# Moving the output-weight sums into the input projection, loading the out projection's first halves one step earlier than their split, and two tiles for kk and v, in a hybrid encoder layer

## The chip, the cores and the metric

The kernel runs on one core of a Trainium2 chip. The metric is the device time of one execution in microseconds, lower being better. The core has five engines that work through queues of their own: TensorE (PE; its weight loads are listed as PEld), VectorE (DVE), ScalarE (ACT), GpSimd (POOL) and SyncE (SP). In this kernel SP issues nearly all the transfers between main memory and the on-chip buffers.

## The reference

One layer over 2048 tokens of width 1024, in fp32. The part that the change touches is the token mixing:

```python
u = rms_norm(h, g_mix_pre[l])
z = u @ w_in[l]
qa, ka, va, qh, fh, ih, gh = jnp.split(z, IN_SPLITS, axis=-1)
ya = swa_with_sinks(qa, ka, va, sinks[l])        # windowed attention, chunks of 64
yh = hgrn2(qh, fh, ih, gh, lb_all[l], hgrn_onorm[l])
y = jnp.concatenate([ya, yh], axis=-1) @ w_out[l]
h = h + rms_norm(y, g_mix_post[l])
...
# cross-attention to 256 memory tokens, then a SwiGLU feed-forward part
```

`hgrn2` is a gated linear recurrence in chunks of 64 tokens with 4 heads of 128:

```python
f = lbf + (1.0 - lbf) * jax.nn.sigmoid(f_logit)
kf = 1.0 - f
b = jnp.cumsum(jnp.log(f) in chunks)
A = einsum(qc * exp(b - b_mid), kc * exp(b_mid - b)), causal
kv = einsum(kc * exp(b_last - b), vc)
S_t = exp(b_last) * S_{t-1} + kv
o = A @ vc + (qc * exp(b)) @ S_prev
output = rms_norm(o, onorm_g) * silu(g)
```

## The kernel before

**Products.** Every fp32 operand is split into a high and a low part, and each product takes three matmuls (L1131, L1132 and L1133 in the big products, L156, L157 and L158 elsewhere). A split is made of a copy to the high part (L987 on ACT, L989 on POOL) and a subtraction for the low part (L990 on DVE). The big products are block products with seven sub-products instead of eight: their operands are sums and differences of blocks of the matrices. The four derived weight combinations of a product (keys 5, 7, 6 and 4) are worked out once by `combined`, which loads blocks, adds or subtracts them on DVE (L1034) and stores the result to main memory with `store` (L78). For the out projection's weights `w_out` they go to the tensor `out_s`: 8 operations of 128 x 1024 elements, because each combination is made in two halves. The big products' schedule is the generator `phases`: it runs over jobs, over their blocks, and over the seven (or fewer) sub-product steps of a block. A job can carry generators that run *beside* its blocks, one step of them after each product step; `put` in `combined` is held behind the newest ACT and DVE instruction at that point.

**Stages.** From 0 to about 250 us `in_first` projects the first 1024 tokens: thirteen pairs of output columns, the first four blocks without combined weights (kinds q, u and v), then nine blocks of seven products. From block 4 on some blocks close with a chain: DVE adds the parts of the output (L644), ACT takes a tanh (L650 or L656), POOL scales (L652), and `decays` takes a logarithm on ACT (L730), which needs another table loaded, and goes on from there. ACT's L1146 copies a partial product out of the accumulator so that PE may go on to the next (PE's L1131 waits for it). Weight tiles come in as `sraw`.

From 250 to about 615 us three generators run in turn, one step of each per pair of token chunks: the windowed attention `swa` (L804 to L853; its last part writes `ys` by L852 on ACT and L853 on DVE, and stores it to `y_d`), the recurrence `hgrn`, and the projection of one column for the second 1024 tokens, `in_proj` (the `cols`). The columns' outputs are the io tiles `z`, of which there are two; they are stored to `z_d`. In the second half of that stage, from pair 8 of the attention on, the generator of the `out_s` sums was run beside these, four steps after each attention pair, with the io tiles `u` and `x` as its two buffers.

From about 615 to 775 us the recurrence's pairs 8 to 15 run beside `fold_cross`, which prepares the cross-attention's weights from the memory (transposes L124 of `raw` weights or memory rows into accumulator banks; L126 on ACT and L127 on DVE copy and split these; L156 to L158 multiply). At each of those pairs one step of the out projection's prologue is taken: from pair 2 on it loaded half of a block of `w_out` into an io tile `z` and split it at once into the out projection's first operands (`T<-z`, L987 on ACT and L990 on DVE). After 775 us come the out projection, the cross-attention and the feed-forward part, all by `phases`.

**A pair of the recurrence.** `hgrn_front` loads k1 (the F columns, for the scores), qq, kk (the F columns again, for the state) and v, each by SP from `z_d`. The scores are L886 on PE, with copies L887 on DVE and L888 on ACT into `atz`. POOL multiplies kk by a decay (L894), PE transposes kk (L897) and v (L902) into banks, and ACT copies them out (kt L899, vt L903 and L904). `hgrn_state` then takes the product L913 of kt and vt, POOL scales the old state (L914), DVE adds (L915); `hgrn_out` is L925 and L926 on PE and L930 to L935 on ACT, POOL and DVE. k1, kk and v had one tile each, qq two.

**Order.** A scheduler with a simulated timeline puts the instructions in an order when the kernel is built; each engine then works through its own list in that order, and SP's list of transfers is in order too. A transfer is issued by SP only when the tile that it fills has been released, and a transfer that waits holds up those behind it in SP's list.

Of the kernel before, what the change touches and what calls it, by code (L numbers as in the profile page):

```python
# [11 lines left out]
F32 = mybir.dt.float32  # L12
# [6 lines left out]
P = 128  # L19
T = 2048  # L20
D = 1024
# [12 lines left out]
C_KA, C_VA, C_QH, C_FH, C_IH, C_GH = 512, 640, 768, 1280, 1792, 2304  # L34
# [14 lines left out]
class Layer:  # L49
# [144 lines left out]
    def mix(self):  # L194
        tc, I = self.tc, self.I
        kw = dict(reuse_waits="tile")
        with contextlib.ExitStack() as left:
            def pool(name, at, **k):
                return at.enter_context(tc.tile_pool(name=name, bufs=1, **k, **kw))

            self.mc = pool("mc", left)
            self.r_x = self.cst.tile([P, NT], F32, name="r_x")
            with (
                tc.tile_pool(name="t1", bufs=3, **kw) as self.ts,
                tc.tile_pool(name="t2", bufs=3, **kw) as self.tb,
                tc.tile_pool(name="s1", bufs=2, side="right", **kw) as self.st_pool,
                contextlib.ExitStack() as at,
            ):
                self.banks(at, "ps1", **MOST)
                self.raws = 3  # L210
                u = self.in_first()
            self.banks(left, "ps2", **FOUR)
            self.hg = pool("hg", left)
            self.wp = pool("wp", left)
            self.io = pool("io", left)
            with tc.tile_pool(name="sw", bufs=1, side="right", **kw) as self.sw:
                self.zero_tiles()
                swa = self.swa(range(NT), lambda n: "st" if n < NPB else "sth")
                hgrn = self.hgrn(range(NPB), "h")
                cols = self.in_proj(1, u)  # L220
                next(cols)
                for _ in range(NPB + 1):
                    next(swa)
                    next(hgrn)
                    next(cols)
                for _ in hgrn:
                    pass
                self.out_sums, side = self.sums("out_s", self.w_out, 4, lambda: self.io_tile("u"), lambda: self.io_tile("x"))
                side = side()
                next(side)  # L230
                pairs = self.hgrn(range(NPB, NT), "gt")
                for i, _ in enumerate(swa, NPB + 2):
                    next(cols)
                    if i == NT + 1 - 0:
                        next(pairs)
                    for _ in range(4):
                        next(side, None)
                for _ in cols:
                    pass
            phases = self.phases(self.jobs(), None, lambda: self.io_tile("z"))  # L240
            with tc.tile_pool(name="xp", bufs=1, side="right", **kw) as self.xp:
                fold = self.fold_cross()
                for _ in range(2):
                    next(fold)
                for i, _ in enumerate(pairs, 1):
                    for _ in range(2):
                        next(fold)
                    if 2 <= i < 10:
                        next(phases)
                for _ in fold:  # L250
                    pass
            left.close()
            with (
                tc.tile_pool(name="t3", bufs=3, **kw) as self.ts,
                tc.tile_pool(name="t4", bufs=3, **kw) as self.tb,
                tc.tile_pool(name="s3", bufs=2, side="right", **kw) as self.st_pool,
                contextlib.ExitStack() as at,
            ):
                self.banks(at, "ps3", **MOST)
                self.raws = 4  # L260
                for _ in phases:
                    pass
# [188 lines left out]
    def in_first(self):  # L451
# [65 lines left out]
        def fetch():  # L517
            for s in range(2):
                for q in range(2):
# [11 lines left out]
                  for i, p in enumerate(self.ORDER)]  # L531
# [1 line left out]
        plain = [b[1:4] + ([],) for b in blocks[:2]]  # L533
        blocks[:2] = ([(k, stream, out, lambda: iter(()), keep) for k, (stream, out, _, keep) in zip("qu", plain)]
                      + [("v", lambda kind: iter([None]), out, after, keep) for _, out, after, keep in plain])
        phases = self.phases([(lambda i, j, a, n: raw[i, j][:, a:a + n, :], 4, blocks, None, {})], T)
        PE, ACT, DVE, POOL = (getattr(mybir.EngineType, e) for e in ("PE", "Activation", "DVE", "Pool"))
        next(phases)
        self.turns("h", 36)
# [45 lines left out]
        u = []  # L585
# [270 lines left out]
    def hgrn_front(self, n, kinds):  # L856
        nc, ph = self.nc, self.hg
        t0 = n * P
        z = self.z_d
        kinds = itertools.cycle(kinds)  # L860

        def get(t, c):
            self.load(t, z[c:c + 512, t0:t0 + P].rearrange("(h p) t -> p h t", p=P))
            return t

        def new(tag, bufs=1, w=P):
            return ph.tile([P, 4, w], F32, tag=tag, name=f"{tag}{n}", bufs=bufs)

        def c8(ap):
            return ap.rearrange("p h (c t) -> p (h c) t", t=64)  # L870

        k1 = get(new("k1"), C_FH)
        qq = new("qq", 2, 192)
        q1 = get(qq[:, :, 0:P], C_QH)
        kk = get(new("kk"), C_FH)
        v = get(new("v"), C_IH)
        g1 = self.G1[:, n, :].unsqueeze(2).broadcast_to([P, 4, 64])

        nc.gpsimd.tensor_tensor(qq[:, :, P:192], qq[:, :, 64:P], g1, ALU.mult)

        at = self.atz[n % 2]
        for i in range(2):
            ps = self.bank(next(kinds))[:, 0:384].rearrange("p (h t) -> p h t", h=2)
            hs = slice(2 * i, 2 * i + 2)
            for r in range(2):
                nc.tensor.matmul(ps[:, r, :], k1[:, 2 * i + r, :], qq[:, 2 * i + r, :], start=True, stop=True)  # L886
            nc.vector.copy_predicated(at[:, hs, :], self.cmask.unsqueeze(1).broadcast_to([P, 2, P]), ps[:, :, 0:P])  # L887
            nc.scalar.activation(at[0:64, hs, 64:P], ps[0:64, :, P:192], AF.Copy)  # L888

        q6 = new("q6", 2)  # L890
        nc.gpsimd.tensor_tensor(q6.rearrange("p h (c t) -> p h c t", t=64), q1.rearrange("p h (c t) -> p h c t", t=64),
                                self.G[:, n, :, :].unsqueeze(3).broadcast_to([P, 4, 2, 64]), ALU.mult)

        nc.gpsimd.tensor_tensor(kk[:, :, 0:64], kk[:, :, 0:64], g1, ALU.mult)  # L894
        ps = self.bank(next(kinds))
        for h in range(4):
            nc.tensor.transpose(ps[:, h * P:(h + 1) * P], kk[:, h, :], self.ident)  # L897
        kt = new("kt")
        nc.scalar.activation(kt, ps.rearrange("p (h t) -> p h t", h=4), AF.Copy)  # L899
        ps = self.bank(next(kinds))  # L900
        for h in range(4):
            nc.tensor.transpose(ps[:, h * P:(h + 1) * P], v[:, h, :], self.ident)  # L902
        vt = new("vt", 2)  # L903
        nc.scalar.activation(vt, ps.rearrange("p (h t) -> p h t", h=4), AF.Copy)  # L904
        return q6, at, kt, vt
# [313 lines left out]
    def phases(self, jobs, first, prologue=None):  # L1219
# [42 lines left out]
        def split(g):  # L1262

            if pending and pending[0][0] <= g:
                _, k, f = pending.pop(0)
                f()
                left[k] -= 1
                return True
            return False

        def half(g, tile):

            if current[0] is None:
                if not queue:
                    return False
                free = min(slots, key=lambda s: s[1])
                if free[1] > g:
                    return False
                n, p, _ = k = queue.pop(0)
                slots.remove(free)  # L1280
                slots.append((free[0], uses[k][-1], free[2]))
                self._n += 1
                dst = (self.big if free[0] == "A" else self.tb).tile(
                    [P, 2, 4, 512], F32R, tag="big" if free[0] == "A" else "T", name=f"T_{self._n}",
                    bufs=4 if free[0] == "A" else 3)[:, :, :jobs[n][1]]
                T[k] = dst
                left[k] = 2
                current[:] = [(k, self.resident(fetch(n, tile), jobs[n][1], p, dst, keep[n], jobs[n][3] is not None)), 0]
            k, f = current[0]
            pending.append((g + lag(k), k, next(f)))  # L1290
            current[1] += 1
            if current[1] == 2:
                next(f, None)
                current[0] = None
            return True
# [28 lines left out]
                made[0] += 1  # L1324

        if not first:
            for i in range(8):
                half(-1, prologue)
                split(len(steps))
                yield  # L1330
        stream(0)
        yield
# [458 lines left out]
```

## Time and profile before

| | us |
|---|---|
| median of 3 runs | 2554.95 |
| lowest and highest | 2553.55 and 2556.43 |
| profiled execution | 2550.01 |
| its span | 2548.3 |
| its mean granted PE clock | 0.997 |

All rows of the profile come from the one profiled execution, which is 4.94 us under the median of the three runs. Names like `psm L1131` give the tile that an instruction writes and its line in the code; `T<-z` reads "T is made from z". Times are microseconds from the start of the span, unless a row gives ns.

### The profile page before, as it was taken

Reading aid. Unit: us, or ns where it says so; the run is one execution under the profiler, and the core shown is the slowest. Engines: PE = TensorE matmul, PEld = TensorE weight load, DVE = VectorE, ACT = ScalarE, POOL = GpSimd, SP = SyncE. Lnnn points to the kernel's source line nnn. Section 1 sums busy time; section 2 is a strip of 40 time slices with the busy share of each in tenths; the row PEclk is TensorE's granted clock in tenths of the full one; section 3 lists DMA queues with packets and bytes.
Section 4 is the critical chain, followed back from the end, with each engine's and each line's share of the span. In section 5 each row is a group of like instructions: output and inputs, shape, how many; then the busy total and the mean of one; then the engine's idle time right before and its main releaser. Section 6 shows DMA issues by size and latency. Waiting matters only on the chain.

```text
span 2548.3 us, 34324 instructions
## 1 busy us (share of the span) xinstructions
PE 2504.8 (98%) x12006; PEld 2092.8 (82%) x12006; DVE 1792.1 (70%) x2871; ACT 1261.6 (50%) x2635; POOL 364.6 (14%) x540
## 2 busy tenths in 40 slices
PE   9999999999999999999999999999999999999998
PEld 8878888877997778878878888888888888878886
DVE  8885488987556989988876555576566557574766
ACT  5553466655555566566753333353333335443543
POOL 4231234321311112102200000000000000000022
PEclk9999999999999999999999999999999999999999
DMA  6455655865887996867954522254465434564786
GB/s 201 146 165 178 192 154 170 230 204 146 259 292 275 316 335 189 274 206 226 333 200 146 177 91 87 74 203 148 160 210 195 144 117 159 180 188 106 228 177 151
DMA packets 387885, 486.33 MB, mean 191 GB/s; under 512 B 22272, under 2 KB 283392, under 8 KB 387712
## 3 DMA queue, kind: packets, MB, share of 16 engines
q1 hardware_dynamic: 381664, 462.12, 55.9%
q0 software_dynamic: 6048, 22.02, 5.0%
q8 instruction: 94, 1.54, 0.2%
q14 instruction: 79, 0.65, 0.1%
HBM read 317.34 MB, written 166.72 MB: 190 GB/s over the span
## 4 chain that ended last, share of the span: by engine, by line
PE 51%; DVE 2%; DMA 1%; issue 1%; ACT 1%; POOL 0%; SPq 0%; DVEq 0%; POOLq 0%; ACTq 0%
PE psm L1133 17%; PE psm L1131 17%; PE psm L1132 17%; DVE T L990 0%; DVE S L990 0%; ACT junk L1504 0%; PE pss L1390 0%; DMA out_dram<-row 0%; DMA row<-d_s 0%; DMA row<-in_w_down_dram 0%; DMA u_d<-row 0%; DMA sraw<-in_w_gate_dram 0%; DVE sum L1106 0%; ACT S L987 0%; ACT T L987 0%
## 5 line engine op out<-in xcount | busy, mean ns | idle before, releaser
L1131 PE MATMUL psm<-T,S 128*128 128x512 f32 x2680 | 1034.1, 390 | 13.3 <-ACT part L1146 7.2
L1132 PE MATMUL psm<-T,S 128*128 128x512 f32 x2680 | 1042.3, 390 | 4.0 <-DVE T L990 3.9
L1133 PE MATMUL psm<-T,S 128*128 128x512 f32 x2680 | 1029.4, 389 | 4.1 <-DVE S L990 4.1
L1131 PEld LDWEIGHTS psm<-T,S 128*128 128x128 f32 x2680 | 503.0, 188 | 125.9 <-ACT part L1146 11.9
L1132 PEld LDWEIGHTS psm<-T,S 128*128 128x128 f32 x2680 | 503.2, 188 | 110.5 <-DVE T L990 7.3
L1133 PEld LDWEIGHTS psm<-T,S 128*128 128x128 f32 x2680 | 503.1, 188 | 110.6 <-DVE S L990 6.3
L987 ACT ACTIVATE S<-sum 128x512 fp32r<-128x512 f32 (+1 forms) x370 | 224.0, 620 | 371.5 <-PE psm L1133 267.3
L990 DVE TENSOR_TENSOR S<-sraw,S 128x512 fp32r<-128x512 f32 (+1 forms) x315 | 211.5, 679 | 218.8 <-ACT S L987 215.8
L1146 ACT ACTIVATE part<-psm 128x512 f32<-128x512 f32 x285 | 168.6, 596 | 251.9 <-PE psm L1133 230.9
L990 DVE TENSOR_TENSOR S<-sum,S 128x512 fp32r<-128x512 f32 (+1 forms) x388 | 257.4, 673 | 42.1 <-ACT S L987 38.3
L987 ACT ACTIVATE S<-sraw 128x512 fp32r<-128x512 f32 (+1 forms) x300 | 184.7, 618 | 110.8 <-PE psm L1133 106.0
L1537 POOL DMA_DIRECT2D y_d<-row x16 | 14.1, 879 | 1077.9 <-DVE row L1721 1027.6
L990 DVE TENSOR_TENSOR T<-row,T 128x1024 fp32r<-128x1024 f32 (+1 forms) x112 | 131.0, 1183 | 30.2 <-ACT T L987 29.2
L157 PE MATMUL psg<-u,whi 128*128 128x512 f32 x320 | 128.3, 401 | 0.0
L158 PE MATMUL psg<-u,wlo 128*128 128x512 f32 x320 | 127.6, 399 | 0.0
L156 PE MATMUL psg<-u,whi 128*128 128x512 f32 x320 | 127.5, 399 | 0.0
L1504 ACT ACTIVATE junk<-row 128x512 f32<-128x512 f32 x160 | 99.6, 624 | 40.6 <-DVE row L1526 20.6
L987 ACT ACTIVATE T<-row 128x1024 fp32r<-128x1024 f32 (+1 forms) x112 | 113.3, 1031 | 7.5 <-DMA row<-d_s 4.3
L1672 DVE TENSOR_TENSOR row<-psm,part 128x512 f32<-128x512 f32 x66 | 43.7, 687 | 66.9 <-PE psm L1133 66.9
L1681 DVE TENSOR_TENSOR part<-psm,part 128x512 f32<-128x512 f32 x66 | 43.8, 687 | 60.1 <-PE psm L1133 59.8
L1721 DVE TENSOR_TENSOR row<-psm,part 128x512 f32<-128x512 f32 x72 | 49.1, 688 | 49.5 <-PE psm L1133 49.4
L814 ACT ACTIVATE S<-S,w_mn 128x256 f32<-128x256 f32 (+1 forms) x128 | 63.0, 496 | 29.6 <-DVE w_mn L810 29.2
(363 smaller groups left out, 3562.2 us busy)
## 6 DMA issues: line engine op xcount, KB each, us to landing
sraw<-in_w_gate_dram SPq DMA_DIRECT2D x44, 512.0 KB, 3.6
sraw<-in_w_up_dram SPq DMA_DIRECT2D x44, 512.0 KB, 3.7
hid_d<-row SPq DMA_DIRECT2D x44, 512.0 KB, 2.7
sraw<-hid_d SPq DMA_DIRECT2D x32, 512.0 KB, 4.2
sraw<-in_w_in_dram SPq DMA_DIRECT2D x44, 256.0 KB, 4.0
z_d<-pair SPq DMA_DIRECT2D x20, 512.0 KB, 3.4
raw<-in_w_in_dram SPq DMA_DIRECT2D x20, 512.0 KB, 4.8
z_d<-z SPq DMA_DIRECT2D x20, 512.0 KB, 4.0
```

The costliest lines, as they stand in the source:

```text
L156: nc.tensor.matmul(ps, ah, bh, start=(i == 0), stop=False)
L157: nc.tensor.matmul(ps, ah, bl, start=False, stop=False)
L158: nc.tensor.matmul(ps, al, bh, start=False, stop=(i == n - 1))
L814: nc.scalar.activation(s[:, r, o:], s[:, r, o:], AF.Exp, bias=mn[:, i:i + 1], scale=-1.0, accum_out=den[:, i:i + 1])
L987: self.nc.scalar.activation(hi, raw, AF.Copy)
L990: self.nc.vector.tensor_tensor(lo, raw, f32(hi), ALU.subtract)
L1131: nc.tensor.matmul(ps, s[:, 0, k, :], t[:, 0, k, :], start=st, stop=False, **kw)
L1132: nc.tensor.matmul(ps, s[:, 0, k, :], t[:, 1, k, :], start=False, stop=False, **kw)
L1133: nc.tensor.matmul(ps, s[:, 1, k, :], t[:, 0, k, :], start=False, stop=sp, **kw)
L1146: nc.scalar.activation(t, ps, AF.Copy)
L1504: self.nc.scalar.activation(junk, a, AF.Square, scale=float(D) ** -0.5, accum_out=to)
L1721: nc.vector.tensor_tensor(d, a, b, ALU.add)
```

## The change

Three edits, with no change to what is computed:

1. The generator of the `out_s` sums leaves the loop of attention and columns. It is now made in `in_first` and given to `phases` as work beside block 4, so that its steps run after the product steps of blocks 4 to 8. Its two buffers are tiles of their own, `wa` and `wb`, one each.
2. The out projection's prologue has nine steps instead of eight: step i loads half i and splits half i − 1. It is driven from the first of the pairs 8 to 15 on (`i < 10`) where it was driven from the second (`2 <= i < 10`), so each split stands in the pair where it stood.
3. kk and v of the recurrence have two tiles each.

```diff
-                self.out_sums, side = self.sums("out_s", self.w_out, 4, lambda: self.io_tile("u"), lambda: self.io_tile("x"))
-                side = side()
-                next(side)
                 pairs = self.hgrn(range(NPB, NT), "gt")
                 for i, _ in enumerate(swa, NPB + 2):
                     next(cols)
                     if i == NT + 1 - 0:
                         next(pairs)
-                    for _ in range(4):
-                        next(side, None)
...
-                    if 2 <= i < 10:
+                    if i < 10:
                         next(phases)
...
+        def weight_tile(tag):
+            self._n += 1
+            return self.st_pool.tile([P, D], F32, tag=tag, name=f"{tag}_{self._n}", bufs=1)
+
+        self.out_sums, side = self.sums("out_s", self.w_out, 4, lambda: weight_tile("wa"), lambda: weight_tile("wb"))
-        phases = self.phases([(lambda i, j, a, n: raw[i, j][:, a:a + n, :], 4, blocks, None, {})], T)
+        phases = self.phases([(lambda i, j, a, n: raw[i, j][:, a:a + n, :], 4, blocks, None, {4: [side]})], T)
...
-        kk = get(new("kk"), C_FH)
-        v = get(new("v"), C_IH)
+        kk = get(new("kk", 2), C_FH)
+        v = get(new("v", 2), C_IH)
...
-            for i in range(8):
-                half(-1, prologue)
-                split(len(steps))
+            for i in range(9):
+                if i < 8:
+                    half(-1, prologue)
+                if i:
+                    split(len(steps))
                 yield
```

## The prediction

> **What bounds the kernel now.** I read the page's busy times first, then the windows by stage, then PE's waits, and then the rows around the work that moves.
>
> ```profile
> span 2548.3 us, 34324 instructions
> ...
> PE 2504.8 (98%) x12006; PEld 2092.8 (82%) x12006; DVE 1792.1 (70%) x2871; ACT 1261.6 (50%) x2635; POOL 364.6 (14%) x540
> ```
>
> TensorE (PE) is busy for 2504.8 of 2548.3 us. The change removes no matmul, so it can win only PE's idle time, 2548.3 − 2504.8 = 43.5 us over the whole span, and time in which PE runs at a lower clock. The recurrence with everything beside it lies between 440 and 775 us:
>
> ```profile
> 440.00:530.00 90.00, 88.73 (x483) 74.77 (x482) 78.62 (x166) 53.52 (x142) 31.67 (x43) 1.00 0.86 251
> 530.00:615.00 85.00, 83.26 (x442) 69.59 (x441) 71.61 (x193) 52.60 (x149) 14.32 (x32) 1.00 0.44 134
> 615.00:660.00 45.00, 41.61 (x296) 38.59 (x295) 28.10 (x38) 24.59 (x52) 6.45 (x8) 0.96 0.90 244
> 660.00:710.00 50.00, 48.13 (x398) 47.15 (x398) 22.63 (x39) 24.88 (x75) 21.85 (x28) 1.00 0.75 241
> 710.00:775.00 65.00, 64.47 (x449) 58.92 (x449) 33.41 (x42) 39.28 (x76) 3.45 (x5) 1.00 0.83 288
> ```
>
> The columns are the stretch, its length, then busy time of PE, weight load, VectorE (DVE), ScalarE (ACT) and GpSimd (POOL), PE's granted clock, the DMA share and GB/s. PE's idle time is 1.27 + 1.74 + 3.39 + 1.87 + 0.53 = 8.8 us: no more than that can be won there, beside the clock of 0.96 in the third row. Which waits make it up, PE's waits tell (first for 615 to 775 us, the last two for 440 to 615 us):
>
> ```profile
> PE pst L902 <- DMA v<-z_d: 2.6, 1, 2.6
> PE pst L902 <- ACT whi L126: 1.1, 1, 1.1
> PE psg L897 <- DVE W L915: 0.8, 2, 0.5
> PE pst L925 <- ACT atz L888: 0.7, 1, 0.7
> ...
> PE psh L849 <- DVE ptl L844: 1.3, 2, 1.0
> PE psh L805 <- DVE ys L853: 0.7, 1, 0.7
> ```
>
> Each line names what waited, what released it, the total, the number of times and the longest.
>
> **Second tiles for kk and v.** With one tile, pair 9's v can only be loaded when pair 8's four transposes at L902 are done. The place in the timeline (PE, then ACT), the windows around it, how long the loads of the tile z take from issue to landing, and a window of the input projection, of which I need the matmuls' pace:
>
> ```profile
> 627.59 0.60 PE L124 MATMUL psh<-ident,u 128*128 128x128 f32 x4
> 630.78 1.04 PE L902 MATMUL pst<-ident,v 128*128 128x128 f32 x4 [2.59 <-DMA v<-z_d]
> ...
> 630.18 1.06 ACT L987 ACTIVATE T<-z 128x1024 fp32r<-128x1024 f32 x1 [3.50 <-DMA z<-in_w_out_dram]
> 631.15 0.58 ACT L126 ACTIVATE mT<-pss 128x512 fp32r<-128x512 f32 x1
> ...
> 628.00:631.00 3.00, 0.41 (x4) 0.25 (x3) 0.53 (x2) 0.81 (x1) 0.00 (x0) 0.98 1.12 231
> 631.00:635.00 4.00, 3.86 (x18) 2.98 (x17) 3.72 (x7) 4.00 (x9) 0.00 (x0) 0.59 0.95 297
> 635.00:640.00 5.00, 5.00 (x46) 5.00 (x45) 2.72 (x4) 1.65 (x10) 3.37 (x5) 1.00 0.95 288
> ...
> DMA to landing us min/median/max: 3.6/5.0/8.3
> ...
> 150.00:200.00 50.00, 49.05 (x216) 40.28 (x215) 38.55 (x55) 21.77 (x36) 14.28 (x19) 1.00 0.60 189
> ```
>
> In the built order of the changed kernel v of pairs 8 and 9 are issued one behind the other on SP, ahead of the last stores of the window attention, so the 2.6 us go. Behind the stall the clock is 0.59 for 4 us, which loses 0.41 × 4 = 1.6 us; at 1.00 again afterwards. Without the stall that loss should go too, but ACT is busy for 4.00 of those 4 us, so PE may meet ACT instead: between 0 and 1.6 us, and I take 1.2, nearer to the clock's row, because the rows after it show PE back at 46 instructions in 5 us. The Trainium skill, "TensorE: Matmul & The Clock Gate", section "What's actually happening", says that the clock halves after an idle window of some 3.4 us; the stall here is shorter, 2.6 us, and the clock fell all the same. By the page's rule alone this term would be 0, and the sum 1.2 us smaller; I go by the row.
>
> What is late next is ACT. In the rows above ACT waits 3.50 us for a loaded weight tile z, and the four copies of L126 stand behind that split. In the new order the second split T<-z stands behind these four copies. The first stands ahead of some 44 projection matmuls, which at 49.05/216 = 227 ns (last row) are 10 us, more than a z load takes (3.6 to 8.3 us), so its wait is covered. But the new order also puts the first L156 of the memory projection ahead of L897: it needs all four L126 copies, 4 × 0.58 = 2.3 us of ACT behind the transposes, while PE has 12 small products and transposes left to run behind the last of these, 1.3 us at 5.00/46 = 109 ns. I charge 0.8 us for that (0 to 2.3).
>
> kk: its multiplication on POOL no longer waits for a load that itself waits for the pair before:
>
> ```profile
> POOL kk L894 <- DMA kk<-z_d: 20.9, 5, 16.6
> ...
> ACT T L987 <- DMA z<-in_w_out_dram: 17.5, 8, 3.7
> ```
>
> The POOL queue holds the state products of L914 behind kk, and DVE's L915 behind those, so the 0.8 us of PE at L897 should go (0 to 0.8). The other 20 us of POOL's waiting hide behind PE already and are worth nothing.
>
> **First halves split a pair late.** The 8 loads, 8 splits on ACT and 8 on DVE stay, in the same pairs; only a load is now issued one step ahead of its split. ACT's 17.5 us of waiting (second row above) mostly go. They cost PE only where a PE wait stands behind them in ACT's queue: the 0.7 us at atz L888, and perhaps the 1.1 us at L126. I take 0.7 (0 to 1.8). SP gets the same 12 transfers, the first still behind the last stores of the projection, because there are two z tiles and the projection's outputs use them.
>
> **The sums, leaving.** Eight additions on DVE, 6 MB of loads and 4 MB of stores leave 440 to 530 us. One of them delays a PE wait visibly:
>
> ```profile
> L1034 DVE TENSOR_TENSOR u<-u,x x6: 1198/1214/1224, 448.1 to 521.9; 128x1024 f32<-128x1024 f32 x6
> ...
> 521.91 1.22 DVE L1034 TENSOR_TENSOR u<-u,x 128x1024 f32<-128x1024 f32 x1 [2.76 <-DMA out_s<-u]
> 523.05 0.68 DVE L853 TENSOR_TENSOR ys<-psh,ys 64x512 f32<-64x512 f32 x1
> ...
> DMA to landing us min/median/max: 2.6/4.2/6.6
> ```
>
> An addition starts at 521.91, and ys of L853, for which PE waited 0.7 us, follows at its end. With the additions gone I count that 0.7, and 0.3 of the 1.27 us idle in 440:530 for the seven others: 1.0 us (0 to 1.3).
>
> **The sums, arriving.** Eight additions of 1.214 us, 9.7 us of DVE, now fall beside blocks 4 to 8 of the input projection, between about 90 and 160 us of the old time. There DVE is the fullest engine after PE:
>
> ```profile
> 90.00:100.00 10.00, 10.00 (x45) 8.27 (x45) 4.52 (x8) 3.76 (x7) 2.65 (x4) 1.00 0.74 225
> ...
> 160.00:170.00 10.00, 9.05 (x40) 7.21 (x39) 10.00 (x13) 8.42 (x13) 5.64 (x5) 1.00 0.62 207
> sum 70.00, PE 66.40 PEld 53.73 DVE 65.31 ACT 45.51 POOL 31.89; mean PE 9.49 PEld 7.68 DVE 9.33 ACT 6.50 POOL 4.56
> ...
> PE psm L1131 <- ACT part L1146: 3.6, 4, 1.2
> ```
>
> The sum row is for 100 to 170 us: DVE 65.31 of 70. By the built order two additions fall before or at 100 us, where DVE has 5.5 us free in ten, and six behind: 65.3 + 6 × 1.214 = 72.6 us in 70. So DVE falls 2.6 us behind and catches up by 200 us, where 11 of the 50 us of the row 150:200 are free. PE's only wait in this stage is the block boundary, 3.6 us over four, and never for a split of DVE: these are made ahead. Only the eighth addition stands directly ahead of a closing addition (L644), through which a boundary's chain runs. So I charge one addition less what its lead hides, +1.0 us. The bounds are −2 us (the new order moves two boundaries' tanh ahead of other ACT work, and half of the 3.6 us could go) and +9.7 us (every addition on the path).
>
> The loads and stores ride SP's queue:
>
> ```profile
> DMA to landing us min/median/max: 2.9/3.5/7.8
> ...
>   DMA sraw<-in_w_in_dram: 2.2, 1
> ...
> L652 POOL TENSOR_SCALAR pair<-pair,fb,fa x8: 1196/1318/2698, 96.0 to 163.0; 128x512 f32<-128x512 f32 x8
> ```
>
> The first row is for the weight tiles sraw between 60 and 200 us; only one engine wait, 2.2 us, was for them. Where a reload of wa or wb waits for a store to land (4.2 us above), the sraw loads behind it in SP's queue wait as well; in the new order one pair of sraw loads stands right behind such a reload. Taken as hidden; without cover it is up to 4.2 us.
>
> **The sum.** −2.6 (v) − 1.2 (clock) + 0.8 (L126 next) − 0.8 (kk) − 0.7 (splits) − 1.0 (sums leave) + 1.0 (sums arrive) = −4.5 us. The profiled execution took 2550.01 us (span 2548.3 and 1.7 around it), 4.94 under the median of 2554.95. So 2545.5 for such an execution, and 2550.4 for the median.
>
> **Rivals.** *A, slower: DVE saturates in the input projection.* For it: DVE at 10.00 of 10 in 160:170, and the boundary operation on POOL, L652, which takes between 1196 and 2698 ns for one shape beside DVE's work. If all eight count, that is +9.7, and four boundaries' POOL operations drawn from 1318 to 2698 ns add 5.5; taking half of the latter, 12.4 − 5.5 (the recurrence's gains) = +7 us, 2562. It turns slower by over 0.2% from (5.5 + 5.1)/1.214 = 8.7 additions' worth, so the additions alone don't do it: the stretched POOL operations or late sraw loads must come on top. Against it: PE never waited for DVE's splits here. The Trainium skill, "SBUF — State Buffer", section "SBUF: two separate sides", says that a DVE operation with two SBUF inputs and a GpSimd operation that reads SBUF exclude each other for their whole length; by that rule the additions stretch POOL's rows, and the spread of L652 agrees.
>
> *B, the waits only move.* v's stall is replaced by ACT's: the first split still blocks ACT's queue for its load, L126 comes later still, and the new L156 waits for it up to 2.3 us. This is also the case that the late split does nothing, since its first load is held by the z tiles. Then about −1 us, 2554.
>
> *C, more.* Half of the boundaries' 3.6 us goes, the full 1.6 of the clock, and the 1.1 at L126: −4.5 − 1.0 − 1.8 − 0.4 − 1.1 = about −8.8, 2546.
>
> **How the numbers follow.** No change means within 0.2%, 5.1 us, about what a measurement of this kernel can tell: 2549.8 to 2560.1. The forecast has 0.43, and lies so near that bound that 0.20 of it counts as faster and 0.23 as same; its own range is 2548 to 2553. C has 0.21 (faster), B 0.16 (same), A 0.20 (slower). Faster 0.41, same 0.39, slower 0.20. The range, 2545 to 2560, takes in C, B and the lower edge of A.
>
> **What would show it.** Right: no wait of L902 for v, the clock at 1.00 around 630 us, idle PE of 440 to 775 us down from 8.8 to about 4.5 us, ACT's wait for z well under 17.5 us, the boundary waits between 75 and 200 us at 3.6 to 5 us. Wrong: PE waiting for a DVE split or an sraw load between 90 and 170 us, L652 above 1.5 us in the median, or a new PE wait for L126 of over 2 us.

## The result: 22 us slower

The changed kernel takes 2576.7 us (median of 6 runs, 2571.25 to 2579.47) against 2554.25 us for the kernel before (6 runs, 2552.34 to 2556.43). The ratio is 1.0085, with a 95% interval from 1.0070 to 1.0099, so it is slower by 18 to 25 us. The forecast was 2550.4, the range 2545 to 2560, with a chance of 0.20 for slower.

The page of the profile after, first its span and busy times:

```profile
span 2577.6 us, 34327 instructions
...
PE 2514.0 (98%) x12006; PEld 2097.7 (81%) x12006; DVE 1792.9 (70%) x2871; ACT 1260.1 (49%) x2635; POOL 363.1 (14%) x540
```

The same 12006 matmuls, but PE's idle time is now 63.6 us instead of 43.5, and its busy time has grown by 9.2 us for the same matmuls, at a lower clock (0.994 in the mean, 0.997 before). Windows of the input projection and of the recurrence after (columns as before: PE, PEld, DVE, ACT, POOL, clock, DMA share, GB/s):

```profile
100.00:150.00 50.00, 42.40 (x176) 34.19 (x175) 38.24 (x51) 23.82 (x36) 15.52 (x19) 0.93 0.75 212
150.00:200.00 50.00, 44.60 (x187) 35.55 (x186) 46.66 (x63) 28.84 (x45) 25.27 (x26) 0.97 0.67 209
...
440.00:530.00 90.00, 89.28 (x507) 76.16 (x506) 77.50 (x181) 57.86 (x166) 33.82 (x52) 1.00 0.47 147
530.00:615.00 85.00, 83.60 (x454) 70.94 (x452) 70.19 (x197) 54.00 (x157) 18.15 (x35) 1.00 0.42 134
615.00:660.00 45.00, 38.33 (x201) 32.84 (x202) 20.83 (x34) 16.67 (x35) 3.27 (x4) 0.96 0.63 186
660.00:710.00 50.00, 47.96 (x396) 47.04 (x396) 28.98 (x42) 26.08 (x66) 16.91 (x22) 1.00 0.77 227
710.00:775.00 65.00, 63.88 (x528) 62.16 (x526) 33.19 (x49) 35.40 (x87) 11.12 (x15) 1.00 0.79 263
```

Between 150 and 200 us PE ran 187 matmuls where it ran 216; its clock there and in the 50 us before is 0.97 and 0.93. Between 440 and 775 us its idle time is 0.72 + 1.40 + 6.67 + 2.04 + 1.12 = 12.0 us, not the forecast 4.5 and more than the 8.8 of before (the kernel is 16 to 22 us behind there, so the windows hold somewhat earlier work).

To see where the time is lost, PE's matmul records are counted in each trace, and the start of the one with a given number is compared with the kernel before. The entries are the lag in us:

| matmul number (its time before) | 400 (73.5) | 1200 (260.4) | 3100 (607.5) | 3500 (669.1) | 4500 (829.1) | last (2539.2) |
|---|---|---|---|---|---|---|
| changed kernel | 5.9 | 19.5 | 16.4 | 21.9 | 24.0 | 29.4 |
| sums alone (e3) | 4.1 | 18.9 | 13.2 | 17.9 | 18.0 | 20.5 |
| additions alone (e5) | 0.1 | 8.0 | 9.3 | 10.5 | 13.8 | 16.7 |
| transfers, tiny additions (e6) | 4.3 | 15.7 | 12.4 | 17.6 | 21.2 | 22.5 |
| the same, first loads held (e15) | −0.2 | 13.5 | 8.7 | 13.6 | 14.9 | 19.3 |
| sums, first loads held (e8) | −0.3 | 12.0 | 7.0 | 11.7 | 15.4 | 17.9 |
| sums at blocks 7 to 11 (e7) | 5.1 | 8.7 | 3.2 | 8.2 | 7.7 | 12.9 |
| tiles alone (e1) | 1.0 | 1.0 | 1.6 | 2.5 | 5.0 | 7.1 |
| late split alone (e2) | 0.1 | −0.3 | −1.5 | −1.0 | 1.3 | 5.0 |

Each row is one execution. The kernels e1, e2, e4 and e9, which leave the input projection as it was, lie within 1.0 us of before in the first two columns. The kernels run some matmuls in another order, but the work done up to a given number agrees within 0.5 us, when each shape is counted with its usual duration. The profiled execution of before was 4.2 us under its median, which is one reason why the last column stands up to 8 us above what the runs give; the part behind 829 us adds between 1.3 and 5.4 us to the lag from row to row. The first four columns are what the argument rests on. In the changed kernel 5.9 us are lost in the first 73 us, 13.6 more in the rest of the input projection, 3.1 come back in the attention and the recurrence's first half, and 5.5 go again between 607 and 669 us.

**The first 73 us.** PE's wait there and SP's timeline after; the last row is SP's timeline before:

```profile
PE psm L1132 <- DVE u L990: 2.1, 1, 2.1
...
18.43 2.21 SPq L75 DMA_DIRECT2D wa<-in_w_out_dram  x2
20.69 0.61 SPq L75 DMA_DIRECT2D wb<-in_w_out_dram  x1
21.49 3.55 SPq L75 DMA_DIRECT2D sraw<-in_w_in_dram  x2
```

```profile
18.26 9.86 SPq L75 DMA_DIRECT2D sraw<-in_w_in_dram  x8
```

The tiles wa and wb are free from the start, so their first loads were put early in SP's list, ahead of and between the input's own weight tiles of this stretch, which are issued from 21.49 instead of 18.26 us. The prediction had not looked at this place.

**The rest of the input projection.** PE's waits (two windows, 100 to 135 and 135 to 200 us), the place of the largest in ACT's timeline, and two windows around it:

```profile
PE psm L1131 <- ACT part L1146: 6.9, 1, 6.9
...
PE psm L1131 <- DVE pair L644: 2.9, 1, 2.9
PE psm L1131 <- ACT part L1146: 1.7, 3, 0.7
PE psm L1131 <- ACT S L987: 1.5, 1, 1.5
...
109.17 1.06 ACT L424 ACTIVATE pair<-pair 128x1024 f32<-128x1024 f32 x1 [6.68 <-DMA pair<-in_x_dram]
...
119.81 0.59 ACT L1146 ACTIVATE part<-psm 128x512 f32<-128x512 f32 x1
...
106.00:119.00 13.00, 7.58 (x34) 5.94 (x32) 7.75 (x11) 6.67 (x9) 4.57 (x5) 0.98 0.42 128
119.00:126.00 7.00, 5.55 (x15) 4.38 (x16) 7.00 (x9) 2.67 (x6) 1.92 (x2) 0.55 0.67 196
```

ACT waits 6.68 us for a load of x rows that the pre-norm of the second tokens squares (L424). Behind it in ACT's queue stand the closing chain of the block (tanh, logarithm with its two table loads) and the copies L1146, for the first of which, started at 119.81, PE waits until 120.45 us. The same square in the kernel before:

```profile
97.56 1.06 ACT L429 ACTIVATE pair<-pair 128x1024 f32<-128x1024 f32 x1 [1.65 <-DMA pair<-in_x_dram]
```

It waited 1.65 us, and PE's wait behind it was 0.50 us. The length of ACT's wait does not decide this alone: one block earlier, where no such chain stands behind the square, ACT waited 6.82 us for its rows in the kernel before (until 80.33 us), and PE did not wait at all.

Behind the stall the clock is 0.55 for 7 us, which takes another 0.45 × 7 = 3 us. By the rows of 0 to 60, 100 to 150 and 150 to 200 us (0.97, 0.93 and 0.97, all 1.00 before) the clock takes 0.03 × 60 + 0.07 × 50 + 0.03 × 50 = 6.8 of the 19.5 us that are lost by 260 us; the rest are waits.

How long transfers take from issue to landing between 70 and 175 us (count, KB each, median us), in the kernel before, then after; below the rows of before stands its window of 100 to 150 us:

```profile
sraw<-in_w_in_dram SPq DMA_DIRECT2D x21, 256.0 KB, 3.6
...
pair<-in_x_dram SPq DMA_DIRECT2D x5, 512.0 KB, 5.0
...
100.00:150.00 50.00, 47.35 (x206) 38.25 (x205) 46.45 (x61) 32.92 (x50) 22.00 (x25) 1.00 0.44 135
```

```profile
sraw<-in_w_in_dram SPq DMA_DIRECT2D x17, 256.0 KB, 6.1
...
pair<-in_x_dram SPq DMA_DIRECT2D x4, 512.0 KB, 6.7
```

**The recurrence.** ACT's two waits for z, PE's wait behind the second, and PE's waits in 615 to 800 us:

```profile
644.17 1.06 ACT L987 ACTIVATE T<-z 128x1024 fp32r<-128x1024 f32 x1 [5.88 <-DMA z<-in_w_out_dram]
...
652.58 1.06 ACT L987 ACTIVATE T<-z 128x1024 fp32r<-128x1024 f32 x1 [3.97 <-DMA z<-in_w_out_dram]
...
654.17 0.69 PE L925 MATMUL pst<-vt,atz 128*128 128x128 f32 x2 [3.72 <-ACT vt L904]
...
PE pst L925 <- ACT vt L904: 5.0, 2, 3.7
PE psg L886 <- DVE z L713: 2.4, 1, 2.4
```

No wait for v is left, but the split of z holds up ACT's queue, and the copy vt behind it now makes PE wait longer than v did.

### The profile page after: what moved, and what is told of

Same layout as the page of the kernel before. It is cut to its first block, busy times and chain, and to the rows that moved or that the text cites. A ratio compares the mean times of both kernels' runs of the same rounds, so it can differ in the third digit from the quotient of the medians.

```text
span 2577.6 us, 34327 instructions
## 1 busy us (share of the span) xinstructions
PE 2514.0 (98%) x12006; PEld 2097.7 (81%) x12006; DVE 1792.9 (70%) x2871; ACT 1260.1 (49%) x2635; POOL 363.1 (14%) x540
## 4 chain that ended last, share of the span: by engine, by line
PE 50%; DVE 2%; ACT 1%; issue 1%; DMA 1%; POOL 0%; SPq 0%; DVEq 0%; POOLq 0%; ACTq 0%
PE psm L1133 17%; PE psm L1131 17%; PE psm L1132 17%; DVE T L990 0%; DVE S L990 0%; ACT junk L1506 0%; PE pss L1392 0%; DMA row<-in_w_down_dram 0%; DMA row<-d_s 0%; ACT T L987 0%; DMA row<-h_d 0%; DVE sum L1106 0%; DMA u_s<-row 0%; DVE row L1636 0%; ACT S L987 0%
## 5 line engine op out<-in xcount | busy, mean ns | idle before, releaser
L1131 PE MATMUL psm<-T,S 128*128 128x512 f32 x2680 | 1037.0, 391 | 23.2 <-ACT part L1146 13.8
L1146 ACT ACTIVATE part<-psm 128x512 f32<-128x512 f32 x285 | 168.3, 596 | 256.3 <-PE psm L1133 225.0
L1506 ACT ACTIVATE junk<-row 128x512 f32<-128x512 f32 x160 | 99.6, 624 | 43.8 <-DVE row L1528 20.4
```

Source lines behind the costliest of these rows:

```text
L1131: nc.tensor.matmul(ps, s[:, 0, k, :], t[:, 0, k, :], start=st, stop=False, **kw)
L1146: nc.scalar.activation(t, ps, AF.Copy)
L1506: self.nc.scalar.activation(junk, a, AF.Square, scale=float(D) ** -0.5, accum_out=to)
```

## The experiments

A difference in us below is the ratio less one, times the 2554 us of before, with its interval.

**One part of the change at a time.** e1 has the two lines for kk and v, e2 the prologue's lines, e3 the moved sums, e4 the first two together. The diffs are those parts of the change.

> The kernel before, with the second tiles for kk and v alone. Theory Q (the loss sits in SP's queue and in ACT's, where waiting transfers and splits hold up what is behind them; the tiles themselves are good): the wait of L902 for v (2.6 us before) goes, with the lower clock behind it, and nothing else moves much: -3 us, between -5 and -1. Rival M (every wait that is removed in the recurrence is replaced by one on ACT's split of z, whatever is edited): between -1 and +3 us, with a new wait of about 2 us or more for ACT in its place.

> The kernel before, with the prologue's loads a step ahead of their splits alone. Theory Q: the z loads still wait for the two z tiles that the last projection columns use, ACT comes to the first splits before the loads have landed and holds up vt behind them: +3 to +8 us. Rival O (the late split is harmless; the waits of the changed kernel at 640 to 655 us come from the order that the moved sums bring about): within 2 us of before.

> The kernel before, with the sums moved to the input projection alone. Theory Q: the loss of the input projection, about 19 us by 260 us of the span, stays whole, and some 2 to 5 us come back where the sums left: +15 us, between +11 and +19. Rival R (most of the change's loss is in the recurrence's edits, and part of the input projection's loss is given back there): less than +8 us.

> The kernel before, with the tiles and the late split, without the move of the sums (the change with its first edit undone). Theory Q: the late split's cost less the tiles' gain: 0 to +6 us, and with the kernel of the sums alone it adds up to the change's +22 us within 4 us. Rival A (the edits work together, so the tiles and the late split bring their gain only once the sums are out of the way, or hurt only then): -3 us or less here, or a sum that misses +22 us by more than 6 us.

Measured: e1 +1.5 us (−0.8 to +3.8), e2 −0.3 (−2.6 to +2.0), e3 +16.1 (12.8 to 19.4), e4 +2.8 (0.5 to 5.1). The sums are most of the loss. e3 and e4 add up to 18.9 of the changed kernel's 21.7, so no working together of the parts is seen within the intervals. The gain of the tiles that I had still expected did not come, and the late split does nothing alone: rival M is right for e1, rival O for e2. In e1's timelines (ACT, DVE, DVE, PE) stands why:

```profile
631.93 1.06 ACT L987 ACTIVATE T<-z 128x1024 fp32r<-128x1024 f32 x1 [3.67 <-DMA z<-in_w_out_dram]
...
633.02 1.22 DVE L990 TENSOR_TENSOR T<-z,T 128x1024 fp32r<-128x1024 f32 x1 [2.91 <-ACT T L987]
634.16 0.68 DVE L915 TENSOR_TENSOR W<-psg,W 128x512 f32<-128x512 f32 x1
...
634.90 0.66 PE L897 MATMUL psg<-ident,kk 128*128 128x128 f32 x4 [4.03 <-DVE W L915]
```

PE no longer stops at L902 for v. It runs on for some operations and stops at L897 for 4.03 us, because the addition L915, which releases its accumulator bank, is queued on DVE behind the split of z, which waits on ACT, which waits 3.67 us for the load of z. The v load and the z load were late at the same time, and taking one away showed the other.

In e3, which has neither the tiles nor the late split, PE's waits of 600 to 800 us have the two of the changed kernel:

```profile
PE pst L925 <- ACT vt L904: 3.3, 2, 2.2
PE psg L886 <- DVE z L713: 2.2, 1, 2.2
```

So these come with the sums' leaving. Without the additions in DVE's list the scheduler runs the attention earlier against the projection's columns. In the kernel before the last stores of the attention (`y_d`) and of the columns (`z_d`) are issued at 626.73 and 628.75 us, in e3 at 630.62 and 645.22. The lag falls by 18.9 − 13.2 = 5.7 us by matmul 3100. Some 1.5 us of this are not the sums': the kernel before has a clock of 0.97 between 250 and 300 us, e3 one of 1.00, and e2 and e9, unchanged up to there, are ahead of it by 1.5 us too. Of the 5.7 us 4.7 are lost again by 3500, where the recurrence's pairs now meet the last columns' outputs and z tiles.

**The additions and the transfers apart.** e5 keeps the old sums and adds eight additions on two scratch tiles (each first filled with zeros) beside blocks 4 to 8. e6 is e3 with additions of 8 of the 1024 columns, which leaves out most of the sums. e15 is e6 with the first loads held back.

```diff
+            wa, wb = weight_tile("wa"), weight_tile("wb")     # e5, a generator beside block 4
...
+                with self.behind():
+                    nc.vector.tensor_tensor(t, t, o, ALU.subtract)
...
-                    nc.vector.tensor_tensor(t, t, o, op)      # e6 and e15, for out_s only
+                    nc.vector.tensor_tensor(t[:, :, 0:4], t[:, :, 0:4], o[:, :, 0:4], op)
```

> The kernel before, with eight extra additions of 128x1024 on two scratch tiles beside blocks 4 to 8 of the input projection, at the steps where the moved sums have theirs, and no extra transfer (the sums stay where they were). Theory Q (the cost is in the transfers, in SP's queue): up to +3 us. Rival D (DVE's saturation between 90 and 170 us is the cost): +8 to +14 us.

> The kernel with the sums alone moved, but each of the eight additions is made on 8 columns of 1024 only, at the same places, with all loads and stores as they are (so most of the sums are left out). Theory Q: still +10 us or more over the kernel before, from +16 with the whole additions. Rival D: +6 us or less.

> The moved sums with all their loads and stores but each addition on 8 columns of 1024 only (most of the sums are left out), and with the first loads held back until block 4. Theory X: the additions play no part, so +10 us or more against the kernel before. Rival D2 (with the additions gone and the early loads held, little is left): +5 us or less.

Measured: e5 +12.3 us (8.9 to 15.3), e6 +19.4 (15.8 to 23.0), e15 +13.0 (10.0 to 16.3). Neither theory alone was right: the additions cost without a transfer, the transfers cost without the additions, and together (e3, +16.1) no more than the transfers. In the table, by matmul 1200, additions have lost 8.0, transfers without the early loads 13.5, both with the early loads held (e8) 12.0. I read this so that both delay the same chain at the block boundaries and the later of the two counts; no run shows that by itself. PE's waits between 75 and 260 us in e5, then in e15 (the copy L1146 of the other kernels has another line number in these), e5's transfers, and ACT's waits for POOL in the kernel before and in e5, with the POOL operation of e5 (there L668 is L652 and L746 is L730 of the others):

```profile
PE psm L1147 <- ACT part L1162: 8.8, 5, 2.5
```

```profile
PE psm L1140 <- ACT part L1155: 12.9, 5, 5.4
```

```profile
sraw<-in_w_in_dram SPq DMA_DIRECT2D x20, 256.0 KB, 3.4
...
pair<-in_x_dram SPq DMA_DIRECT2D x5, 512.0 KB, 4.8
...
150.00:200.00 50.00, 45.30 (x184) 36.84 (x185) 40.30 (x54) 23.61 (x39) 13.99 (x19) 0.93 0.50 148
```

```profile
ACT pair L730 <- POOL pair L652: 4.8, 4, 1.5
...
ACT pair L746 <- POOL pair L668: 8.3, 4, 2.7
...
L668 POOL TENSOR_SCALAR pair<-pair,fb,fa x8: 770/1754/3286, 96.1 to 169.9; 128x512 f32<-128x512 f32 x8
```

In the kernel before this wait is 4.1 us over five in the same window. In e5 the loads land as fast as before (3.4 and 4.8 us), so its longer stalls come from the engines: the POOL operation of the chain has a median of 1754 ns where it had 1318, and ACT's logarithm waits 3.5 us longer for it, just ahead of the stalls. PE waits 4.7 us longer, and its clock of 0.93 between 150 and 200 us takes 3.5 us: together 8.2, about the lag of 8.0. In e15 it is the other way round, with x rows landing in 6.2 us and sraw in 5.6 (medians of the same view).

**Holding the first loads, and moving the sums further.** e8 is e3 with a write of 8 columns by DVE into each tile at block 4, which its first load has to wait for. e7 puts the sums beside block 7, e11 does both.

```diff
-..., 4, blocks, None, {4: [side]})], T)       # e7, e11
+..., 4, blocks, None, {7: [side]})], T)
...
+                with self.behind():             # e8, e11: once for each of wa and wb
+                    nc.vector.memset(t[:, 0:8], 0.0)
```

> The sums alone moved, with the first load of each of their two tiles held back by a write of 8 columns on DVE at block 4, so that SP's queue has no load of these ahead of the input's first weight tiles. Theory Q: the 4 to 5 us that were lost by 60 us of the span come back, the rest of the loss stays: +9 to +13 us against the kernel before. Rival E (the lateness of the first 60 us is made up for later, since PE would wait at the same block boundaries anyway): +14 to +18 us as without the hold.

> The sums alone moved, but beside blocks 7 to 11 instead of 4 to 8, where DVE has more room (31.4 of 50 us busy in the kernel before between 200 and 250). Theory Q: the first loads still stand ahead of the input's weight tiles, which keeps about 4 to 5 us; the rest of the input projection's loss falls from 14 to about 5, and 4 come back in the recurrence: +3 to +9 us. Rival D: 0 to +3 us.

> The sums alone moved, beside blocks 7 to 11, and with the first loads of their two tiles held back until block 7. Theory Q, with parts that add up: 5 us less than beside blocks 7 to 11 without the hold (+11.5), so +5 to +8 us against the kernel before. Rival E (the early loads' loss is made up for anyway): +10 to +13 us.

Measured: e8 +15.6 us (12.3 to 18.6), e7 +12.5 (8.9 to 16.1), e11 +8.7 (5.6 to 11.7). The hold takes the lag at matmul 400 from 4.1 to −0.3, and at 1200 from 18.9 to 12.0, as theory Q has it, but the runs of e8 show next to nothing of it: +15.6 lies above what Q expected (+9 to +13), though its interval reaches into that, and within what rival E expected (+14 to +18), although the lag at 1200 speaks against E's reason. Where it goes again is seen in the table (11.7 by 3500, 15.4 by 4500), and why is not settled. e7 and e11 lose less where DVE has room, but e7 more than either theory expected; e11 lies between what Q (+5 to +8) and E (+10 to +13) expected and decides nothing. The two differ by 3.8 us, with overlapping intervals. None of these is faster than the kernel before.

**The z tiles.** e9 is the kernel before with three io tiles z, e10 the changed kernel with three, e12 is e11 with three.

```diff
-... bufs=3 if tag == "x" else 2)
+... bufs=3 if tag in ("x", "z") else 2)
```

> The kernel before, with three io tiles z instead of two and nothing else. Theory Z (in the recurrence's second half the out projection's first weight loads wait for the z tiles of the last projection columns; ACT's splits wait for them and hold up what is behind): ACT's wait for z falls from 17.5 us to 12 or less. Since PE is held there by v (2.6 us) and not by ACT, the time changes little: -2 to +1 us. Rival N (the loads are bound by the transfers themselves): ACT's wait stays above 15 us.

> The changed kernel with three io tiles z instead of two. Theory Z: its new waits between 640 and 660 us (PE for vt of L904, 5.0 us, and for z of L713, 2.4 us) go, with ACT's two waits for z before them: -4 to -8 us against the changed kernel, so +14 to +18 us against the kernel before. Rival N (these waits come from the order alone, in which the attention ends some 10 us earlier than the projection's columns): within 2 us of the changed kernel.

> As the run before it (sums beside blocks 7 to 11, first loads held back), and with three io tiles z. Theories Q and Z together: the recurrence keeps the 5 to 6 us that it gains by 600 us where the sums leave, less 0 to 2 at 640: 0 to +3 us against the kernel before, perhaps below it. Rival N: +5 to +8 us, as without the third tile.

Measured: e9 +2.0 us (−0.3 to +4.1), e10 +20.4 (17.4 to 23.5), e12 +10.5 (7.4 to 13.8). ACT's wait for z in e9, then ACT's for z and PE's for vt in e10, all between 602 and 800 us:

```profile
ACT T L987 <- DMA z<-in_w_out_dram: 15.1, 5, 5.3
...
ACT T L987 <- DMA z<-in_w_out_dram: 11.7, 6, 4.5
...
PE pst L925 <- ACT vt L904: 0.9, 1, 0.9
```

In e9 ACT's wait fell only from 17.5 to 15.1 us, where theory Z had 12 or less and rival N over 15: in the kernel before the third tile does little. In the changed kernel it lets ACT's wait fall from 18.8 us to 11.7 and PE's wait for vt from 5.0 us to 0.9. So there the z tiles are what held up vt. But the time moves by 1.3 us only, within the intervals: PE's wait for z of L713 rose from 2.4 to 3.7 us, and of the 5.5 us that the changed kernel loses between matmul 3100 and 3500, 2.2 remain. That is what rival N expected of the time (within 2 us), and e12 lies above what either expected (0 to +3, +5 to +8). Theory Z names the wait of the changed kernel rightly and not its worth.

**The x rows by another queue.** e13 is the changed kernel, e14 the kernel before, with the rows of x issued by POOL instead of SP.

```diff
-                self.load(t[:, 0, :], self.I["x"][...])
+                nc.gpsimd.dma_start(t[:, 0, :], self.I["x"][...])
```

> The changed kernel with the rows of x for the second tokens' pre-norm loaded by GpSimd's queue instead of SP's. Theory X (in the input projection the large stall of 6.9 us comes from a load of x that is late because SP's queue has the sums' loads and stores ahead of it; ACT's square waits for it with the partial products' copies behind it): the stall for part of L1146 falls from 6.9 us to under 2 and the time by 5 to 9 us against the changed kernel, so +13 to +17 us against the kernel before. Rival D2 (DVE's additions delay the same chain anyhow): within 3 us of the changed kernel.

> The kernel before with the rows of x loaded by GpSimd's queue, as a control. Both theories: within 2 us of before, unless GpSimd's issue of the loads delays its own work at the block boundaries (+2 to +4 us).

Measured: e13 +22.2 us (18.9 to 25.8), e14 +4.3 (2.0 to 6.6). The square of the same block in e13, and how long these loads take:

```profile
108.35 1.06 ACT L424 ACTIVATE pair<-pair 128x1024 f32<-128x1024 f32 x1 [5.95 <-DMA pair<-in_x_dram]
...
pair<-in_x_dram POOLq DMA_DIRECT2D x5, 512.0 KB, 6.5
```

The stall of that block falls from 6.9 to 3.0 us, but two more, of 3.2 and 3.3 us, follow at 136 and 160 us, and even set against its control e13 is still 18 us slower, as rival D2 expected. This does not settle theory X, since e13 hardly moved the load: the rows were issued 0.7 us earlier (101.75 against 102.45) and the square started 0.8 us earlier (108.35 against 109.17). In POOL's queue the load stands behind a split copy (L989) that waited 5.16 us for PE.

What comes before the load in the changed kernel is seen in SP's timeline. SP does not wait just before it. The load ends a run of transfers that starts at 95.83 us with the stores of the rows before (`un_d`, which waited for their transpose), and in which the store of `wa` and two loads of `wb` now stand. From the first of these stores to the load it is 6.6 us, where it was 5.2, and the rows then took 6.7 us to land, where they took 5.6. So a delay of one block's rows can return in the next block's, by the order of the list. That loop is read from the timelines; no run cut it, and none separates the place in the list from the landing time.

## Why the prediction was wrong

**Sums arriving, +1.0 (bounds −2 to +9.7): the step that failed.** The sums alone (e3) cost 16.1 us, and 18.9 us of lag had built up by the end of the input projection. Three things in the working were wrong.

First, DVE's spare time was taken as a buffer: 72.6 us of work in 70, caught up later. But PE does not run against DVE's average. It runs against the chain that closes a block, which goes DVE, ACT, POOL, ACT, DVE, and the additions lie between its parts. Additions alone (e5) lose 8.0 us by the end of the input projection, where the term had +1.0: 4.7 us of longer waits and 3.5 us of clock, which the term did not have at all. Over the whole kernel e5 has +12.3 us (8.9 to 15.3), an interval that holds the bound of 9.7; where the part behind the input projection comes from is open. "PE never waited for DVE's splits here" was true and beside the point.

Second, the transfers were taken as hidden, up to 4.2 us. They cost 13.0 us (e15) without whole additions and without the early loads, as much as the additions cost alone. I had looked for sraw loads behind a store in SP's queue. What happened was that the loads of that stretch landed later (medians of sraw 3.6 to 6.1 us, of x rows 5.0 to 6.7 us), while the DMA share between 100 and 150 us rose from 0.44 to 0.75, and that the sums' transfers stand ahead of the x rows in SP's list. The loads of the x rows were not looked at, though ACT's square of them stands ahead of the copies PE waits for.

Third, the early loads of wa and wb ahead of the input's own tiles, 4 to 6 us by 73 us, were not in the sum. What they are worth over the whole kernel is not shown, since e8 without them has +15.6.

**Sums leaving, −1.0.** Larger and then undone: e3 gains 5.7 us by matmul 3100, some 4 of them by the sums' leaving, and loses 4.7 by 3500. The change of order that the removal brings was not in the sum.

**v, −2.6, and the clock, −1.2.** The wait for v went, and nothing was gained: e1 has +1.5 us (−0.8 to +3.8). This is rival B, to which I gave 0.16, with the mechanism that it named (the split of z blocks ACT's queue for its load) and another place (L915 on DVE and L897 on PE for e1, vt in the changed kernel). My cover for the first split, 44 projection matmuls, was of the changed kernel's order, and there the load of z was issued only at 638.63 us and landed at 644.09.

**Late split, −0.7.** Not to be told from zero (e2, −0.3 ± 2.3); ACT's wait for z in the changed kernel is 18.8 us, where 17.5 were said to mostly go. The note that the first load is still held by the two z tiles was the right one.

**kk, −0.8, and the L126 copies, +0.8.** Too small to be seen here.

**Rival A** had the sign and the place, but its mechanism only in part. The stretched POOL operations did not come in the changed kernel:

```profile
L652 POOL TENSOR_SCALAR pair<-pair,fb,fa x8: 772/1203/2648, 102.6 to 178.9; 128x512 f32<-128x512 f32 x8
```

The median is 1203 ns against 1318 before. In e5 they did come, with 1754 ns and 3.5 us more of ACT's waiting, so the mechanism is there when the additions stand alone, and "the additions alone don't do it" was wrong: e5 is slower by more than 0.2%. Rival A's chance of 0.20 was too low, since the price of what the additions bring along, 20 loads and 8 stores in the stretch where DVE is fullest, was left out of it.

Still open are whether the transfers act by their landing time or by their place in SP's list, the 1.3 to 5.4 us that the lag grows behind matmul 4500 in all the rows of the table (also in those of kernels that are no slower over their runs), and where e8's regained time goes.

## What to carry to other kernels

Work that moves into another stage brings its transfers along, and here the loads of that stage came later for it: read the order and the landing times of the loads there, and which engine's queue has one of them at its head. An engine with idle time is no cover when a chain through it sets the pace; count the moved operations against the chain's waits. When a stall goes, look at what else is landing at that moment: here v and z were late together, and removing the wait for one gained nothing.

## What the runs showed of the hardware

In these traces the granted clock fell behind stalls of PE. Behind the stall of 6.9 us it was 0.55 for 7 us, and in the prediction's rows 0.59 for 4 us behind one of 2.6 us. In e1, with the stall of 4.03 us at 631 to 635 us, the next 5 us ran at:

```profile
635.00:640.00 5.00, 4.49 (x26) 4.25 (x27) 3.78 (x7) 2.67 (x9) 0.37 (x1) 0.66 1.04 314
```

So each of these three stalls cost another 1.6 to 3.2 us of clock, and a sum over waits alone is too small by that. The length of a stall does not tell it for certain: e5's stalls of 2.5 and 2.3 us at 150 and 173 us were followed by a lower clock (0.93 over 150 to 200 us), and the changed kernel's of 2.5 us at 1134 us was not (1.00 over 1136 to 1146 us).
